# A hybrid transformer block on one core: an even pace for the stream in the scans, the MLP weight's scale two iterations ahead, the MLP's first products ahead of the last norm

## The chip, the cores and the metric

The kernel runs on one core of one Trainium2 chip. Its engines are TensorE (PE; its weight loads are PEld), VectorE (DVE), ScalarE (ACT), GpSimd (POOL) and SyncE (SP, which here issues the DMAs). The metric is the device time of one execution in microseconds (us); less is better.

## The reference, cut to what matters

One layer over 2048 latent tokens and 256 context tokens, with a width D of 1024 and float32 inputs. One projection feeds three mixers (gated linear attention, RWKV-7, retention); their outputs go through one projection, and a squared-ReLU MLP with 4096 hidden columns follows.

```python
zl = modulate(rms_norm(xl, norm1_g), ml[0], ml[1]) @ w_in      # and the same for the context
yl_gla, yl_rwkv, yl_ret = gla_mixer(...), rwkv7_mixer(...), retnet_mixer(...)
xl = xl + ml[2] * (concatenate([yl_gla, yl_rwkv, yl_ret], -1) @ w_out)
hl = modulate(rms_norm(xl, norm2_g), ml[3], ml[4])
xl = xl + ml[5] * (square(relu(hl @ mlp_w1)) @ mlp_w2)
return rms_norm(xl, final_norm_g)
```

## The kernel before

**Stages.** The input projection and the features of RWKV-7 come first (to about 610 us), then the scans (to 2091), the output projection (to 2316) and the MLP.

**The scans** are put in order by a planner, `Order` (L1041). Each piece of work is a generator, a stream with a position that runs from `first` to `last` over `count` yields. `pick` takes, among the streams that are ready by the planner's own clock, the one with the lowest position; one that is more than `lead` ahead of the lowest waits. A yield of a number says how long the stream waits for other engines, and a yield of a function is a condition. The streams are `prepare` and `chains` (RWKV-7's blocks and recurrences), `finish`, `inputs`, `mix` (the heads of the gated attention, then two pairs of retention heads, `ret_pair`, L1654), the finishing of a head, which `follow` (L1776) adds as a stream of its own, and `ip_stream` (L447). The last does what the input projection left open: five groups of columns (`STREAM_T`: V of the attention, its gates, q, k and v of retention pair 0, the same of pair 1, the gates of retention), 16 or 18 token tiles each; a tile is 24 matmuls in four pieces, an eviction (L480) and a store to `zt`. It always is ready, and its positions run from 0 to 312 over 345 pieces. `k.streamed` counts its finished groups. `ret_pair` waits for `streamed >= 3 + p2`; the finishing of a retention pair waits for `streamed >= 5`, all of it. The second pair doesn't begin its queries before the first pair's finishing is done.

**The MLP** takes the tokens in two halves of 1024. Each half has 16 iterations (`fp`) over 256 hidden columns. `hidden` makes seven products `pu` of 12 matmuls each (L2041; a Strassen scheme over 2 x 2 blocks of tokens and columns, `PRODUCTS`), combines them on ScalarE and VectorE (L2049 to L2060), and takes relu and square (L2065, L2066), from which it makes a high and a low part, `uh` and `ul`. Then, for each of 8 token tiles, 12 matmuls into `pz` (L2105) and two sums into `acc` (L2107). In the first half `mlp_w1` (L1857) makes the weights: two loads of 512 KB (`st`, L1866), the largest absolute value (L1867, and across partitions in `over_partitions`: a transpose into `pmx`, L1850, a maximum `mx`, L1852, and a matmul that spreads it, L1853), the scale `s`, and for each product a sum of blocks (`ws`), the high part (L1879), the low part (L1880) and a store to `w1d` (L1881). In the second half they are read back from `w1d`. `wo` has 7 buffers, and the banks of `pu` and `pmx` are four together (pool `mlp1`). `mlp_w2` (L1894) loads and scales the second weight (L1899 to L1905).

**Between them**, `out_proj` (L1918) closes with `norms(7)`, the last two token tiles' norm, then W2, and returns; iteration 0's `hidden` is called in `mlp` (L2025). `norms(7)` works in tiles of the pools `opx` and `opy`; `acc` (pools `mla0` and `mla1`) and `mlx` are opened when these are closed, while `mlu`, `mlw2` and `mlw` lie on the other side of the memory. `norms` for the first 8 token tiles, which is what `hidden` of the first half reads, are done long before.

A scheduler orders each engine's instructions when the kernel is built, with program order as priority, and it moves an instruction ahead of one that isn't ready.

Of the kernel before, what the change touches and what calls it, by code (L numbers as in the profile page):

```python
# [22 lines left out]
P = 128  # L23
# [420 lines left out]
STREAM_T = [TV, TG[0:3], RET_T[0], RET_T[1], TG[3:5]]  # L444


def ip_stream(k, wp, ps):  # L447
# [10 lines left out]
    for g, cols in enumerate(STREAM_T):  # L458
# [4 lines left out]
        for ti in range(2 if kind == "g" else 0, NT):  # L463
# [577 lines left out]
class Order:  # L1041

    def __init__(self, nc):
        self.nc, self.t, self.streams, self.mode = nc, 0.0, [], None

    def add(self, gen, first, last, count, lead=1e9):
        s = Stream(gen, first, last, count, lead)
        s.ready = self.t  # L1050
        self.streams.append(s)
        return s
# [28 lines left out]
    def run(self):  # L1081
# [572 lines left out]
def ret_pair(k, p2, pool, ps):  # L1654
# [6 lines left out]
    nc.sync.dma_start(V.rearrange("p c h n -> p c (h n)"), grp(0, T, vc))  # L1661
# [4 lines left out]
    def keys(t0, n):  # L1666
        c0, nch = t0 // P, n // P
        if t0:
# [13 lines left out]
    yield 4  # L1682
    kd = keys(*TOKB[0])
    yield 4
    for bi, (t0, n) in enumerate(TOKB):
# [15 lines left out]
        if bi + 1 < len(TOKB):  # L1701
            kd = keys(*TOKB[bi + 1])
# [70 lines left out]
    k.fin = follow(k, 5, finish_rows(k, pool, ps, Y, ms, 2, 64, gc, k.col("rng", p2), 768 + 128 * p2))  # L1773


def follow(k, n, gen):  # L1776
# [6 lines left out]
    return k.order.add(steps(), k.mix.pos() - 20, k.mix.pos() + 5, 10)  # L1783


def mixers(k, ps):
# [3 lines left out]
    with tc.tile_pool(name="mix", bufs=1) as mp:  # L1790
# [55 lines left out]
def over_partitions(k, ps, pool, x):  # L1846

    nc = k.nc
    pt = ps.tile([P, 512], F32, tag="p1", name="pmx")
    nc.tensor.transpose(pt[0:1, 0:P], x, k.ident)  # L1850
    m = pool.tile([1, 1], F32, tag="mx1", name="mx1")
    nc.vector.tensor_reduce(m, pt[0:1, 0:P], axis=AX.X, op=ALU.max)  # L1852
    nc.tensor.matmul(pt[:, P : P + 1], k.ones[0:1], m, start=True, stop=True)  # L1853
    return pt[:, P : P + 1]


def mlp_w1(k, fp, sp, tag, bufs, ws, wp, eng):  # L1857

# [404 lines left out]
```

## Time and profile before

| | us |
|---|---|
| median of 3 runs | 3725.27 |
| lowest, highest | 3703.3, 3731.29 |
| the profiled execution | 3744.08 |
| span of its trace, first to last instruction | 3742.3 |

In the rows a line such as `pz<-w2h,uh` names the tile written and the tiles read. Idle time stands before the instruction that ended it, with what released it. The granted clock (PEclk) is TensorE's share of 2.4 GHz; it has two levels, 1.2 and 2.4 GHz, and a share between them is a mean over a stretch.

### The profile page before, as it was taken

How to read it: one execution, taken by the hardware profiler on the slowest of the kernel's cores; microseconds unless marked ns; L12 is line 12 of the kernel's file. 1: busy time of each engine (PE TensorE's matmuls, PEld its weight loads, DVE VectorE, ACT ScalarE, POOL GpSimd, SP SyncE). 2: the span in 40 equal slices, each digit the busy share in tenths (PEclk: the TensorE clock that was granted, in tenths of full speed). 3: DMA queues.
4: the chain of work that ended last, by engine and by line, in shares of the span. 5: the costliest groups of instructions: out<-in, count | busy, mean ns of one | idle time of the engine just before them, and what ended most of it. 6: DMA issues, size and time to landing. Idle time of an engine off the chain costs nothing. (4 is left out here: it accounts for less than half of the span.)

```text
span 3742.3 us, 62893 instructions
## 1 busy us (share of the span) xinstructions
PE 3411.3 (91%) x23616; PEld 2272.0 (61%) x23616; DVE 2437.2 (65%) x5128; ACT 1394.9 (37%) x3097; POOL 685.7 (18%) x863
## 2 busy tenths in 40 slices
PE   6798999999998999989998598899999999999997
PEld 2444446676666766767776486555555556666665
DVE  7458785668856576674665488876777665444446
ACT  3355553344436255252434234333333342112113
POOL 3224443234413222222332100000000010000001
PEclk7898998988978799778888799999999999999998
DMA  7988876446634436333332387633333365223222
GB/s 228 202 229 252 249 214 198 133 135 191 163 115 126 104 105 153 76 102 104 96 98 84 136 201 258 218 130 123 125 124 124 111 184 186 89 89 119 89 89 97
DMA packets 534217, 547.09 MB, mean 146 GB/s; under 512 B 276475, under 2 KB 407366, under 8 KB 533134
## 3 DMA queue, kind: packets, MB, share of 16 engines
q1 hardware_dynamic: 533904, 542.99, 48.7%
q8 instruction: 188, 3.08, 0.4%
q14 instruction: 125, 1.02, 0.1%
HBM read 331.18 MB, written 187.55 MB: 139 GB/s over the span
## 5 line engine op out<-in xcount | busy, mean ns | idle before, releaser
L2041 PE MATMUL pu<-H,wo 128*128 128x512 f16 x2688 | 623.9, 386 | 23.9 <-ACT wo L1879 20.8
L2107 DVE TENSOR_TENSOR acc<-acc,pz 128x512 f32<-128x512 f32 x512 | 348.0, 686 | 376.2 <-PE pz L2105 372.8
L2041 PEld LDWEIGHTS <-wo 128*128 128x128 f16 x2688 | 254.2, 99 | 357.1 <-issue 58.4
L2105 PE MATMUL pz<-w2h,uh 128*128 128x512 f32 x1024 | 441.2, 431 | 26.0 <-ACT uh L2068 23.9
L2105 PE MATMUL pz<-w2l,uh 128*128 128x512 f32 x1024 | 411.4, 402 | 0.0
L2105 PE MATMUL pz<-w2h,ul 128*128 128x512 f32 x1024 | 396.8, 396 | 0.0
L1065 PE MATMUL pz<-rwh,rh 128*128 128x384 f16 (+1 forms) x1376 | 289.3, 342 | 8.5 <-DMA rh<-hd 5.9
L2120 POOL TENSOR_TENSOR acc<-acc,fg 128x1024 f32<-128x1024 f32 x10 | 24.0, 2416 | 1457.6 <-ACT acc L2119 1457.6
L1065 PEld LDWEIGHTS <-rh 128*128 128x128 f16 x2064 | 198.0, 105 | 134.6 <-issue 37.5
L2105 PEld LDWEIGHTS pz<-w2h,uh 128*128 128x128 f32 x1024 | 199.9, 195 | 83.6 <-ACT uh L2068 26.1
L2105 PEld LDWEIGHTS pz<-w2l,uh 128*128 128x128 f32 x1024 | 199.9, 195 | 41.4
L2105 PEld LDWEIGHTS pz<-w2h,ul 128*128 128x128 f32 x1024 | 195.8, 191 | 43.3
L2065 ACT ACTIVATE u<-u 128x512 f32<-128x512 f32 x64 | 36.8, 622 | 476.5 <-DVE s L2059 476.5
L425 PEld LDWEIGHTS <-wh 128*128 128x128 f16 (+2 forms) x1072 | 111.0, 107 | 151.1 <-issue 44.6
L425 PE MATMUL pz<-hT_hi,wh 128*128 128x512 f16 (+5 forms) x536 | 127.2, 379 | 42.0 <-ACT zs L428 23.8
L2053 ACT ACTIVATE s<-pu,iv 128x512 f32<-128x512 f32 x96 | 65.5, 686 | 259.3 <-PE pu L2041 258.0
L1065 PE MATMUL pz<-rwl,rh 128*128 128x384 f16 (+1 forms) x688 | 143.7, 339 | 0.0
L1065 PE MATMUL pg<-Z,BK 64*128 64x128 f32 (+1 forms) x864 | 138.4, 339 | 4.0 <-issue 1.9
L1988 PE MATMUL pz<-woh,yh 128*128 128x512 f32 x256 | 100.2, 406 | 28.2 <-DMA x<-in_w_out_dram 21.6
L1065 PEld LDWEIGHTS pg<-Z,BK 64*128 64x128 f32 x864 | 115.8, 233 | 16.8 <-issue 5.8
L425 PE MATMUL pz<-hT_hi,wl 128*128 128x512 f16 (+5 forms) x536 | 122.8, 366 | 0.0
L425 PE MATMUL pz<-hT_lo,wh 128*128 128x512 f16 (+5 forms) x536 | 121.0, 363 | 0.0
(526 smaller groups left out, 6915.8 us busy)
## 6 DMA issues: line engine op xcount, KB each, us to landing
rh<-hd SPq DMA_DIRECT2D x86, 512.0 KB
st<-in_mlp_w_dram SPq DMA_DIRECT2D x64, 512.0 KB
w1d<-wo SPq DMA_DIRECT2D x112, 256.0 KB
wo<-w1d SPq DMA_DIRECT2D x112, 256.0 KB
x<-in_x_dram SPq DMA_DIRECT2D x32, 512.0 KB
mw<-in_mod_w_dram SPq DMA_DIRECT2D x32, 512.0 KB
w2d<-w2h SPq DMA_DIRECT2D x32, 512.0 KB
w2d<-w2l SPq DMA_DIRECT2D x32, 512.0 KB
```

Of the source, the lines that this page charges most:

```text
L425: nc.tensor.matmul(pz[:M, o : o + step], a[:, kk, 0:M], b[:, kk, t0 + o : t0 + o + step], start=(i == 0), stop=(i == 23))
L1065: return op(out, lhs, rhs, **kw)
L1988: nc.tensor.matmul(pz, a[:, kk], w[:, kk, 512 * hf : 512 * hf + 512], start=(kk + i == 0), stop=(kk == KD - 1 and i == 2))
L2041: nc.tensor.matmul(bank, W[o][:, a, kk], H[o][:, 4 * b + kk], start=(i == 0), stop=(i == 11))
L2053: nc.scalar.activation(s, product(o), AF.Copy, scale=iv)
L2065: nc.scalar.activation(r, r, AF.Relu)
L2105: nc.tensor.matmul(pz, U[q][tb][u][:, ts], W2[q][w][:, cs], start=(i == 0), stop=(i == 5))
L2107: nc.vector.tensor_add(a[:, cs], a[:, cs], pz)
L2120: nc.gpsimd.tensor_mul(a, a, fg)
```

## The change

There are three parts. *The scans*: the gates of retention come fourth and the second retention pair fifth in `STREAM_T`. The stream has a period of 3.1 us of the planner's clock in place of positions: when its next piece is due it goes first; when no other stream is ready it may go up to three periods early. `ret_pair` loads V with the keys, block by block, and waits for the stream's tiles block by block (`there`), not for whole groups; the finishing waits for 4 groups in the first pair and 5 in the second, and its positions begin 10 later. *The scale*: `mlp_w1` is cut in two. `mlp_w1_load` loads the weight two iterations ahead and makes its scale from the sum of squares (on ScalarE, with a matmul that sums across partitions in `norm_scale`, L334); `mlp_w1` is now a generator that makes one product's weight behind each token tile of the iteration before. *The first products*: `hidden` is now `mlp_hidden`, and iteration 0's is called in `out_proj` ahead of W2, and W2 ahead of `norms(7)`; iteration 1's weight is loaded into `mlx`.

```diff
-STREAM_T = [TV, TG[0:3], RET_T[0], RET_T[1], TG[3:5]]
+STREAM_T = [TV, TG[0:3], RET_T[0], TG[3:5], RET_T[1]]
 def ip_stream(k, wp, ps):
...
+            k.tile = ti + 1
             yield 0
-        k.streamed += 1
+        k.streamed, k.tile = k.streamed + 1, 0
...
     def pick(self):
         open_ = [s for s in self.streams if s.cond is None or s.cond()]
+        paced = [s for s in open_ if s.period and s.ready <= self.t]
+        for s in paced:
+            if s.due <= self.t or len(open_) == 1:
+                return s
+        if len(open_) > 1:
+            open_ = [s for s in open_ if not s.period] or open_
         head = min(s.pos() for s in open_)
         near = [s for s in open_ if s.pos() <= head + s.lead] or open_
         ready = [s for s in near if s.ready <= self.t]
         if ready:
             return min(ready, key=Stream.pos)
+        for s in paced:
+            if s.due <= self.t + 3 * s.period:
+                return s
...
+            if s.period:
+                s.due = max(s.due, self.t - s.period) + s.period
...
 def ret_pair(k, p2, pool, ps):
-    nc.sync.dma_start(V.rearrange("p c h n -> p c (h n)"), grp(0, T, vc))
...
     def keys(t0, n):
+        nc.sync.dma_start(V[:, c0 : c0 + nch].rearrange("p c h n -> p c (h n)"), grp(t0, n, vc))
...
-    yield 4
+    def there(i):
+        t0, n = TOKB[i]
+        return lambda: (k.streamed, k.tile) >= (2 + 2 * p2, (t0 + n) // P)
+    yield there(0)
     kd = keys(*TOKB[0])
-    yield 4
+    yield 8
...
         if bi + 1 < len(TOKB):
+            yield there(bi + 1)
             kd = keys(*TOKB[bi + 1])
...
-    k.fin = follow(k, 5, finish_rows(...))
+    k.fin = follow(k, 4 + p2, finish_rows(...))
...
-    return k.order.add(steps(), k.mix.pos() - 20, k.mix.pos() + 5, 10)
+    return k.order.add(steps(), k.mix.pos() - 10, k.mix.pos() + 15, 10)
...
-                yield lambda: k.streamed >= 3 + p2
                 yield from ret_pair(k, p2, pool, ps)
...
-def mlp_w1(k, fp, sp, tag, bufs, ws, wp, eng):
+def mlp_w1_load(k, fp, sp, tag, bufs, jp):
...
         nc.sync.dma_start(st[h], w1v[h, :, :, 256 * fp : 256 * fp + 256])
-        nc.vector.tensor_reduce(am[:, h : h + 1], st[h], axis=AX.XY, op=ALU.max, apply_absolute_value=True)
-    nc.vector.tensor_max(am[:, :1], am[:, :1], am[:, 1:])
-    nc.vector.tensor_scalar(ar, over_partitions(k, k.p1, sp, am[:, :1]), 1e-30, 2.0 ** -14, ALU.max, ALU.mult)
-    nc.vector.reciprocal(s, ar)
-    nc.vector.tensor_mul(iv, ar, k.h_inv2)
+        sq = jp.tile([P, D], BF16, tag="sq", name="sq", bufs=1)
+        nc.scalar.activation(sq.rearrange("p (k n) -> p k n", k=4), st[h], AF.Square, accum_out=am[:, h : h + 1])
+    nc.vector.tensor_add(am[:, :1], am[:, :1], am[:, 1:])
+    s, ar = norm_scale(k, k.p1.tile([P, 512], F32, tag="p1", name="pnrm")[:, 0:1], k.w1s, am[:, :1])
+    nc.vector.tensor_mul(k.iv[:, fp : fp + 1], ar, k.h_inv2)
+    return st, s
+def mlp_w1(k, fp, st, s, sp, ws, wp, eng):
     for o in PRODUCTS:
...
         nc.sync.dma_start(k.w1d[fp, o], w)
+        yield o, w
...
 def out_proj(k, es, H, hp):
...
+        U0 = mlp_hidden(k, H, up, W0, k.iv[:, 0:1])
         k.g2 = mod_row(k, w2, 3)
+        W2 = [mlp_w2(k, q, w2) for q in range(2)]
         norms(7, xs, ss[:, 14:16])
-        W2 = [mlp_w2(k, q, w2) for q in range(2)]
...
 def mlp(k, H, hp, es, U0, W2, up, w2p, wp0):
...
+        loaded = None if half else mlp_w1_load(k, 1, wp, "st", 2, wp)
         for fp in range(NF):
...
-                W1 = mlp_w1(k, fp, (wp, wp0)[fp % 2], "st", 2, 1, k.w1, nc.vector)
                 W2 = [mlp_w2(k, 2 * fp + q, w2p) for q in range(2)]
-            U = hidden(*W1)
+            U = mlp_hidden(k, H, up, W1, k.iv[:, fp : fp + 1]) if fp or half else U0
+            following = iter(()) if half or fp == NF - 1 else mlp_w1(k, fp + 1, *loaded, (wp, wp0)[(fp + 1) % 2], 1, k.w1, nc.vector)
+            if not half and fp < NF - 2:
+                loaded = mlp_w1_load(k, fp + 2, (wp0, wp)[fp % 2], "st", 2, wp)
+            W1 = {}
             for t in range(8):
...
                     nc.vector.tensor_add(a[:, cs], a[:, cs], pz)
+                W1.update([x for x in (next(following, None),) if x])
...
-            k.order.add(ip_stream(k, fp, fps), 0, 312, 345, 4)
+            k.order.add(ip_stream(k, fp, fps), 0, 312, 345, period=3.1)
```

## Rows read from the trace of the kernel before

**Rows 1.** The page's first part: busy us (share of the span) x instructions.
```profile
PE 3411.3 (91%) x23616; PEld 2272.0 (61%) x23616; DVE 2437.2 (65%) x5128; ACT 1394.9 (37%) x3097; POOL 685.7 (18%) x863
```

**Rows 2.** Windows by stage: from:to, length, busy us (instructions) of PE, PEld, DVE, ACT, POOL, granted clock, DMA.
```profile
612.00:2030.00 1418.00, 1320.29 (x13955) 974.29 (x13954) 945.08 (x2549) 596.82 (x1692) 427.49 (x589) 0.86 0.44 123
2030.00:2091.00 61.00, 43.86 (x282) 37.20 (x282) 20.72 (x43) 19.50 (x37) 17.51 (x16) 0.75 0.14 43
...
2316.00:2386.00 70.00, 54.12 (x226) 32.14 (x225) 62.16 (x101) 29.59 (x47) 0.00 (x0) 0.91 0.80 269
2386.00:3006.00 620.00, 563.33 (x2382) 354.34 (x2382) 438.88 (x666) 199.34 (x315) 0.00 (x0) 0.93 0.38 131
...
3075.00:3695.00 620.00, 620.00 (x2782) 399.35 (x2780) 309.93 (x464) 135.00 (x239) 7.50 (x3) 1.00 0.33 113
```

**Rows 3.** Waits of PE, 2386 to 3006: us in total, times, longest us.
```profile
PE pmx L1853 <- DVE mx L1852: 24.6, 13, 2.5
PE pu L2041 <- ACT wo L1879: 20.6, 6, 3.5
PE pz L2105 <- ACT uh L2068: 12.4, 8, 1.6
```

**Rows 4.** Timeline of PE at two iterations' boundaries: start, us, instruction, [idle before].
```profile
2574.23 0.38 PE L1853 MATMUL pmx<-mx,ones 1*128 1x1 f32 x2 [2.49 <-DVE mx L1852]
2578.11 5.46 PE L2041 MATMUL pu<-H,wo 128*128 128x512 f16 x16 [3.50 <-ACT wo L1879]
...
2583.64 0.39 PE L2105 MATMUL pz<-w2l,uh 128*128 128x512 f32 x1
2583.87 0.40 PE L2105 MATMUL pz<-w2h,uh 128*128 128x512 f32 x1
...
2622.36 0.38 PE L1853 MATMUL pmx<-mx,ones 1*128 1x1 f32 x2 [1.96 <-DVE mx L1852]
2624.39 0.79 PE L2105 MATMUL pz<-w2h,uh 128*128 128x512 f32 x1 [1.65 <-ACT uh L2068]
2624.98 0.63 PE L2105 MATMUL pz<-w2l,uh 128*128 128x512 f32 x1
2625.41 0.63 PE L2105 MATMUL pz<-w2h,uh 128*128 128x512 f32 x1
...
2629.90 0.40 PE L2105 MATMUL pz<-w2h,uh 128*128 128x512 f32 x1
```

**Rows 5.** Window between two boundaries of the first half, columns as in Rows 2.
```profile
2624.40:2667.40 43.00, 43.00 (x181) 27.48 (x181) 29.73 (x46) 9.92 (x15) 0.00 (x0) 0.94 0.41 141
```

**Rows 6.** DVE's lines, 2386 to 3006 (busy, mean ns); ScalarE's line L1995 (min/median/max ns).
```profile
L1867 DVE TENSOR_REDUCE am<-st 128x1 f32<-128x1024 f32 x25 | 30.4, 1217 | 9.1 <-DMA st<-in_mlp_w_dram 8.6
...
L1995 ACT ACTIVATE sq<-x x16: 1040/1057/1062, 2137.3 to 2318.1; 128x1024 bf16<-128x1024 f32 x16
```

**Rows 7.** Timeline of SP and DVE: a load of `st` and its reduction.
```profile
2589.18 0.38 SPq L1866 DMA_DIRECT2D st<-in_mlp_w_dram  x1
...
2592.83 1.22 DVE L1867 TENSOR_REDUCE am<-st 128x1 f32<-128x1024 f32 x1 [0.69 <-DMA st<-in_mlp_w_dram]
```

**Rows 8.** Timeline of PE, SP and DVE in the first MLP iteration.
```profile
2333.44 0.80 PE L2105 MATMUL pz<-w2h,uh 128*128 128x512 f32 x1 [8.36 <-ACT uh L2068]
...
2358.86 0.34 SPq L1961 DMA_DIRECT2D h<-hl  x1
...
2361.46 1.92 SPq L2097 DMA_DIRECT2D acc<-x  x4
...
2366.71 1.28 DVE L2107 TENSOR_TENSOR acc<-acc,pz 128x512 f32<-128x512 f32 x2 [2.20 <-DMA acc<-x]
```

**Rows 9.** Line L480 (min/median/max ns, first and last start); timeline of PE in the tail.
```profile
L480 ACT ACTIVATE rzs<-pz,siv x238: 348/368/413, 605.4 to 2021.7; 128x128 f32<-128x128 f32 x119
...
2032.41 1.12 PE L1065 MATMUL fpt<-ident,rY 128*128 128x128 f32 x4 [3.03 <-POOL rY L1463]
...
2083.63 1.11 PE L1065 MATMUL fpt<-ident,rY 128*128 128x128 f32 x4 [7.70 <-POOL rY L1463]
```

More of the change, by code (lines that the diff above doesn't have):

```diff
@@ L1046, in __init__, with add @@
         self.nc, self.t, self.streams, self.mode = nc, 0.0, [], None
-    def add(self, gen, first, last, count, lead=1e9):
+    def add(self, gen, first, last, count, lead=1e9, period=None):
         s = Stream(gen, first, last, count, lead)
-        s.ready = self.t
+        s.ready = s.due = self.t
+        s.period = period
         self.streams.append(s)
@@ L1772, in ret_pair @@
         yield 2
-    k.fin = follow(k, 5, finish_rows(k, pool, ps, Y, ms, 2, 64, gc, k.col("rng", p2), 768 + 128 * p2))
+    k.fin = follow(k, 4 + p2, finish_rows(k, pool, ps, Y, ms, 2, 64, gc, k.col("rng", p2), 768 + 128 * p2))
 def follow(k, n, gen):
@@ L1843, in summed @@
     return out
[L1846 to L1854, printed above, removed]
-def mlp_w1(k, fp, sp, tag, bufs, ws, wp, eng):
+def mlp_w1_load(k, fp, sp, tag, bufs, jp):
     nc = k.nc
@@ L1890, in mlp_w1_kept @@
         k.nc.sync.dma_start(W[o], k.w1d[fp, o])
-    return W, k.iv[:, fp : fp + 1]
+    return W
 def mlp_w2(k, ft, wp):
@@ L1915, in mlp_w2_kept, with mlp_hidden, product, new @@
     return vh, vl
+def mlp_hidden(k, H, up, W, iv):
+    nc = k.nc
+    def product(o):
+        bank = k.p1.tile([P, 512], F32, tag="p1", name="pu")
+        i = 0
+        for a, b in ((0, 0), (1, 0), (0, 1)):
+            for kk in range(4):
+                nc.tensor.matmul(bank, W[o][:, a, kk], H[o][:, 4 * b + kk], start=(i == 0), stop=(i == 11))
+                i += 1
+        return bank
+    def new(nm):
+        return up.tile([P, 512], F32, tag=nm, name=nm, bufs=1)
+    def add(out, o, s):
+        nc.vector.scalar_tensor_tensor(out, product(o), iv, s, ALU.mult, ALU.add)
+    s1, s2, s3 = (new(nm) for nm in ("s1", "s2", "s3"))
+    for o, s in ((1, s2), (2, s3), (0, s1)):
+        nc.scalar.activation(s, product(o), AF.Copy, scale=iv)
+    u10, u01 = new("u10"), new("u01")
+    add(u10, 3, s2)
+    add(u01, 4, s3)
+    nc.vector.tensor_sub(s3, s3, s2)
+    nc.vector.tensor_add(s1, s1, s3)
+    nc.vector.tensor_sub(s2, u10, u01)
+    nc.vector.tensor_add(s2, s2, s1)
+    add(s2, 6, s2)
+    add(s1, 5, s1)
+    U = [[], []]
+    for q, r in ((1, u10), (0, u01), (0, s2), (1, s1)):
+        nc.scalar.activation(r, r, AF.Relu)
+        nc.scalar.activation(r, r, AF.Square)
+        uh = up.tile([P, 512], F32R, tag="uh", name="uh")
+        nc.scalar.copy(uh, r)
+        ul = up.tile([P, 512], F32R, tag="ul", name="ul")
+        nc.vector.tensor_tensor(ul, r, uh.bitcast(F32), ALU.subtract)
+        U[q].append((uh, ul))
+    return [U[0][::-1], U[1]]
 def out_proj(k, es, H, hp):
@@ L2031, in mlp @@
     ps = es.enter_context(tc.tile_pool(name="mlps", bufs=4, space=PSUM))
-    def hidden(W, iv):
-        def product(o):
-            bank = k.p1.tile([P, 512], F32, tag="p1", name="pu")
-            i = 0
-            for a, b in ((0, 0), (1, 0), (0, 1)):
-                for kk in range(4):
-                    nc.tensor.matmul(bank, W[o][:, a, kk], H[o][:, 4 * b + kk], start=(i == 0), stop=(i == 11))
-                    i += 1
-            return bank
-        def new(nm):
-            return up.tile([P, 512], F32, tag=nm, name=nm, bufs=1)
-        def add(out, o, s):
-            nc.vector.scalar_tensor_tensor(out, product(o), iv, s, ALU.mult, ALU.add)
-        s1, s2, s3 = (new(nm) for nm in ("s1", "s2", "s3"))
-        for o, s in ((1, s2), (2, s3), (0, s1)):
-            nc.scalar.activation(s, product(o), AF.Copy, scale=iv)
-        u10, u01 = new("u10"), new("u01")
-        add(u10, 3, s2)
-        add(u01, 4, s3)
-        nc.vector.tensor_sub(s3, s3, s2)
-        nc.vector.tensor_add(s1, s1, s3)
-        nc.vector.tensor_sub(s2, u10, u01)
-        nc.vector.tensor_add(s2, s2, s1)
-        add(s2, 6, s2)
-        add(s1, 5, s1)
-        U = [[], []]
-        for q, r in ((1, u10), (0, u01), (0, s2), (1, s1)):
-            nc.scalar.activation(r, r, AF.Relu)
-            nc.scalar.activation(r, r, AF.Square)
-            uh = up.tile([P, 512], F32R, tag="uh", name="uh")
-            nc.scalar.copy(uh, r)
-            ul = up.tile([P, 512], F32R, tag="ul", name="ul")
-            nc.vector.tensor_tensor(ul, r, uh.bitcast(F32), ALU.subtract)
-            U[q].append((uh, ul))
-        return [U[0][::-1], U[1]]
     NF, ENDS = DFF // 256, (1, 3, 5, 7)
@@ L2224, in tile_hybrid_block @@
             fps = es.enter_context(tc.tile_pool(name="iprps", bufs=1, space=PSUM, side="right"))
-            k.order, k.inputs, k.streamed, k.fin = Order(nc), 0, 0, None
+            k.order, k.inputs, k.streamed, k.tile, k.fin = Order(nc), 0, 0, 0, None
             rw_scan(k, bp, ps)
```

15 lines of the change are left out of this document (6 added, 9 removed).

## The prediction

> **What bounds the kernel now.** The page comes first: TensorE is busy for 91% of the span and VectorE for 65% [rows 1], so TensorE's waits and its clock decide, and the question is in which stage it waits. The table of windows by stage answers that [rows 2]. In the second half of the MLP TensorE is busy for all of 620 us at a granted clock of 1.00 (2.4 GHz) and issues 2782 matmuls: 620 / 2782 = 0.2229 us each. One iteration is 84 products into `pu` and 96 into `pz`, 180 x 0.2229 = 40.1 us. The first half computes the same with weights that it makes itself, and 13 of its iterations take the 620 us from 2386 to 3006: 47.7 us each, at a clock of 0.93. The 13 x 7.6 = 98.4 us between the two halves are the largest sum in reach. The waits of that stretch say where they lie: 24.6 us before `pmx` on `mx`, 20.6 before `pu` on `wo`, 12.4 before `pz` on `uh`, 57.6 in all, 4.4 an iteration [rows 3]. The timeline shows that they all stand at one place, between the last product of an iteration and its first `pz` [rows 4]: TensorE waits 2.49 us for the maximum and then 3.50 for the scaled weight, or, every second time, 1.96 and 1.65. After it the matmuls start 0.43 us apart, which is the 1.2 GHz level, where later ones start 0.23 apart: 13 of them take 2624.39 to 2629.90, 5.5 us in place of 2.9. So a boundary costs 4.4 us of idle time, 0.7 of `pmx` work and 2.6 of slow clock. Between two boundaries nothing else holds TensorE: 181 matmuls fill 43.0 of 43.0 us with VectorE at 69% [rows 5].
>
> In the scans TensorE is busy for 1320 of 1418 us, and then comes a tail of 61 us with 43.9 us of work [rows 2]. The stream's last eviction starts at 2021.7; only then does the first retention pair's finishing start (`fpt` at 2032.41), the second pair's queries wait for that, and its own finishing is the last thing, behind a wait of 7.7 us [rows 9].
>
> **The change part by part.** *The scale.* Two reductions on VectorE, 1.217 us each [rows 6], go, with the maximum across partitions. In their place stand two squares with a sum on ScalarE, the same operation on a tile of the same size as L1995, 1.06 us [rows 6], one small matmul (as `pmx`, 0.5 us) and seven VectorE operations on one column for five that go. Per iteration VectorE falls from 438.9 / 13 = 33.8 us to about 31.5, and ScalarE rises from 199.3 / 13 = 15.3 to about 17.5, with 41 us to do it in [rows 2]: hidden. If they weren't, ScalarE's 2.1 us would be the price. What counts is where the chain stands. It was load, maximum, two matmuls, scale, weight, product; now the scale of iteration n+2 is asked for at the head of n, and the weights of n+1 are made behind each token tile's `pz`. A load takes 3.65 us from issue to the reduction that waited for it [rows 7], and the 96 `pz` take 96 x 0.2229 = 21.4, so the weight is there when the last product of n ends, and the first products of n+1 can fill the wait for `uh`. That is how the second half runs, with weights loaded ahead and no wait at all [rows 2]. Of the 98.4 us I keep 0.5 x 13 = 7 for the small matmul and 0.5 x 13 = 6 for waits that stay, between 0.1 (43.0 - 2.6 slow - 181 x 0.2229 [rows 5]) and the 1.65 of `uh` [rows 4]. The term is **-85**, with bounds -75 to -92.
>
> *The first iteration.* Its products now stand ahead of the last norm and of the weight W2. TensorE waited 8.36 us for `uh` there [rows 8], since VectorE did norm and W2 work in between; 4.0 us (from the end of the last product, 2622.36 - 1.96, to `pz` at 2624.39 [rows 4]) is what that chain takes undisturbed: gain 4.4. Against it: the norm comes later, and what lies where its tiles lay comes later too. Before, the loads of token tiles 4 to 7 of `acc` are issued at 2361.46, right behind the norm's last store at 2358.86, and VectorE waits for them until 2366.71 [rows 8]. TensorE filled that time with the next iteration's products, because their weights were in the pool `mlw`. Now the weights of iteration 1 are loaded into `mlx`, which opens when the norm's pools close. With 8 sums done and 4 banks full, TensorE has 72 `pz` (16 us) before it must stand: from about 2333.4 - 4.4 + 16 + 2.6 = 2348 to between 2359 (8 us of VectorE work on the next weight are out of the norm's way) and 2367. After that 24 `pz` and 84 products, 24 us, lead to 2383 to 2391 and, with a wait for the new scale, some us more, where before the next `pz` block began near 2386. I take **+4**, with bounds -8 and +20: nearer the lower end, as the upper one needs a norm that gains nothing.
>
> *The scans.* The stream's matmuls stay the same; they come every 3.1 us of the planner's time and, between, where nothing else is ready. The gates of the retention heads are streamed ahead of the second pair, so the first finishing no longer waits for the whole stream, and the second pair's queries run beside the recurrences. No price row exists for a new order. Bounds: the tail's 61 us can at best shrink to the last finishing, 2075.9 (2083.63 - 7.70) to 2091, 15 us: -46; with its 43.9 us of work set among holes that are all too short it gains 61 - 44 = 17; and a worse pace can lose. The largest waits for the stream's own loads are a few us, so I bound the loss by the idle time growing by a quarter of 98 us: +25. I take **-25**, near the middle of the gains. Eight more loads of V stand on SP's queue, under 0.5 us each (four `acc` loads took 1.92 [rows 8]), over 200 us: hidden; 4 us if not.
>
> The sum is -85 + 4 - 25 = -106 on the execution of 3744.08 us (span 3742.3). That execution is 0.5% above the median of the runs, 3725.27; off the median the forecast is **3619 us**.
>
> **The rivals.** *The gap stays.* If no weight or no free bank of the four in `p1` is there when the last product ends, TensorE waits 4.0 us for `uh` and starts slowly, as now every second time; idle time changes by 0.4 us an iteration, 5 in all: 3725 - 5 + 4 - 25 = 3699. For it: the scale's tile takes one of the four banks just there. Against: the second half has the same four banks and no gap [rows 2]. The Trainium skill, "Perfetto Trace Analysis" (Identifying the Most-Contended Engine), says that a gap which repeats can mean too few buffers for the next tile; by that rule the gap would stay and the sum be this rival's.
>
> *VectorE paces.* 31.5 us at the 69% that it reached beside a full TensorE [rows 5] would make an iteration of 45.6 us, a gain of 27: 3677. Against: from 2316 to 2386 it was busy for 62.2 of 70 us [rows 2].
>
> *The stream's pace loses*: +25 in place of -25: 3669.
>
> *The other side: the small matmul waits.* It stands in TensorE's queue behind the last product. If the tile's two loads began only there, TensorE would stand for 2 x 3.65 + 2 x 1.06 + 0.15 = 9.6 us and start slowly: 40.1 + 0.5 + 0.5 + 2.6 + 9.6 = 53.3 an iteration, +73: 3725 + 73 + 4 - 25 = 3777. With the other two terms it is slower by 1% from a wait of 8.4 us on. Against: the tiles are free once the weights of n are made, a whole product block (84 x 0.2229 = 18.7 us) earlier. By the Trainium skill, "TensorE: Matmul & The Clock Gate" (Part 2, Step-by-step), matmuls stay in program order and only weight loads are pulled ahead, so such a wait could not be stepped over; the trace agrees, with 2.49 us of nothing before `pmx` [rows 4].
>
> **How the numbers follow.** Less than 1% (37 us) can't be told from no change: the three runs lie 28 us apart. Likeliest, as summed: 0.62, from 3725 - 92 - 8 - 46 = 3579 to about 3665 (MLP -75, first iteration +20, scans -5). VectorE paces 0.12 (3677), the stream's pace loses 0.09 (3669), the gap stays 0.09 (3699), the small matmul waits 0.04 (3777), something worse in the scans 0.04. Below 3688 lie the first three and a little of the fourth: faster 0.85, same 0.10, slower 0.05. The range 3572 to 3682 leaves out the last three and the fringe of the first, under 0.2.
>
> **What would show it.** Right: in the first half an iteration near 41 us at a clock of 1.00, no wait before the small matmul, and `pu` matmuls between the last product and the first `pz`; `fpt` rows of the first pair well before the stream's last eviction, and a tail under 45 us; a new wait of some 10 us on `acc` near 2350. Wrong: boundaries that still show `pz` waiting 4 us for `uh` with matmuls 0.43 us apart behind, or more idle time in the scans than 98 us.

## The result, and the profile after

| | before | after |
|---|---|---|
| median of 4 runs, us | 3716.55 | 3631.61 |
| lowest, highest, us | 3703.3, 3731.29 | 3604.11, 3642.57 |
| the profiled execution, us | 3744.08 | 3641.55 |
| its span, us | 3742.3 | 3639.4 |

The ratio is 0.9743, with a 95% interval of 0.9687 to 0.9800: faster by 117 to 74 us, 96 in the middle, where 106 were forecast. The sum was close. Its terms were less so: two of them erred by 15 and 12 us against each other, and the third, that of the scans, came out right by luck, for a wrong reason.

The page's first part, after (for [rows 1]):
```profile
PE 3362.6 (92%) x23600; PEld 2257.2 (62%) x23600; DVE 2388.7 (66%) x5128; ACT 1427.0 (39%) x3161; POOL 685.8 (19%) x863
```
Windows by stage of after, columns as in [rows 2]: the scans, their tail behind the stream's last eviction, the first MLP iteration, the first half, the second half:
```profile
612.00:2073.80 1461.80, 1357.18 (x14237) 1011.04 (x14235) 963.87 (x2595) 615.66 (x1732) 447.06 (x605) 0.84 0.43 120
1980.00:2073.80 93.80, 76.24 (x372) 64.24 (x372) 43.87 (x134) 27.03 (x59) 19.96 (x20) 0.51 0.14 42
...
2315.90:2385.00 69.10, 46.03 (x187) 29.67 (x188) 51.92 (x88) 27.21 (x44) 0.00 (x0) 0.85 0.81 258
2385.00:2915.00 530.00, 529.87 (x2389) 341.11 (x2389) 403.79 (x661) 223.15 (x362) 0.00 (x0) 1.00 0.42 147
3000.00:3620.00 620.00, 616.28 (x2756) 403.11 (x2754) 307.33 (x465) 135.30 (x240) 4.75 (x2) 1.00 0.29 98
```
The fourth of these lines is the main result. TensorE is busy for 529.87 of 530 us at a granted clock of 1.00, where [rows 2] had 563 of 620 at 0.93. None of the waits of [rows 3] is left, and neither is the slow start behind them [rows 4]. The third line is the price: 46 us of work in 69.1 us. These are the longest waits of TensorE from 2300 to 2385 (us in total, times, longest):
```profile
PE pnrm L338 <- DMA acc<-x: 13.2, 1, 13.2
PE pnrm L338 <- DVE am L1876: 8.8, 1, 8.8
PE pz L2123 <- ACT uh L1965: 7.3, 1, 7.3
```
And this is where the first two stand on TensorE's timeline:
```profile
2335.43 0.39 PE L2123 MATMUL pz<-w2h,ul 128*128 128x512 f32 x1
2349.06 0.56 PE L338 MATMUL pnrm<-am,ones 128*128 128x1 f32 x2 [13.24 <-DMA acc<-x]
...
2374.71 1.03 PE L1938 MATMUL pu<-H,wo 128*128 128x512 f16 x4
2384.49 0.59 PE L338 MATMUL pnrm<-am,ones 128*128 128x1 f32 x2 [8.75 <-DVE am L1876]
```
`pnrm` is the new small matmul that makes a scale; twice TensorE stands before it. The view names the loads of `acc` as what ended the first wait, but the matmul's own input `am` was written only then too, on VectorE's timeline:
```profile
2348.80 0.16 DVE L1876 TENSOR_TENSOR am<-am 128x1 f32<-128x1 f32 x1 [0.48 <-ACT sq L1875]
```
Nothing behind this matmul could have run either: the next `pz` needed a bank that the sums into `acc` freed from 2348.91 on, and iteration 1's products need the weights that this very scale makes. So the first wait is iteration 1's weight coming late. SyncE's timeline says why. It shows the two loads of iteration 2's weight at 2300.72 and the two of iteration 1's, the one that is wanted first, at 2340.07, when the norm's tiles are closed:
```profile
2300.72 1.82 SPq L1873 DMA_DIRECT2D st<-in_mlp_w_dram  x2
...
2340.07 0.98 SPq L1873 DMA_DIRECT2D st<-in_mlp_w_dram  x2
2341.09 2.58 SPq L2115 DMA_DIRECT2D acc<-x  x4
```
To compare stages, the table counts the 5760 `pu` and `pz` matmuls of the MLP, of which the traces of these kernels hold all, and takes the time at the 85th, at the 265th and at the 2881st, where half of them are done. The 85th is the first `pz` in every kernel but first_back, where products of iteration 1 come ahead of it. The table covers before, after, scans_only and the experiments that touch the MLP. All stages are in us; "w_out" is the start of TensorE's wait of some 22 us for that weight, where the scans end.

| kernel | scans end (w_out) | to the 85th | 180 matmuls on | 2616 matmuls on | to the end |
|---|---|---|---|---|---|
| before | 2091.2 | 242.2 | 52.4 | 688.0 | 668.5 |
| after | 2073.8 | 242.1 | 69.0 | 587.5 | 667.0 |
| scans_only | 2045.2 | 241.2 | 53.3 | 683.6 | 668.2 |
| mlp_only | 2065.5 | 240.2 | 66.5 | 586.1 | 670.9 |
| first_back | 2065.6 | 287.2 | 40.5 | 585.4 | 667.1 |
| w1_in_mlw | 2042.9 | 244.6 | 59.7 | 585.5 | 669.3 |
| w2_late | 2060.7 | 246.5 | 48.4 | 589.7 | 667.0 |
| one_ahead | 2052.0 | 238.3 | 69.1 | 681.8 | 667.3 |
| weights_at_head | 2059.4 | 243.0 | 68.2 | 587.5 | 665.4 |
| max_two_ahead | 2058.6 | 245.6 | 69.9 | 606.0 | 671.0 |

Between before and after: -17.4 in the scans, +16.6 - 0.1 around the first iteration, -100.5 in the first half, -1.5 behind it, together -102.9, the difference of the spans. 2616 matmuls are 14.5 iterations, so one takes 47.3 us before and 40.4 after.

### The profile page after: what moved, and what is told of

Read it like the earlier page. It is cut to its first block, busy times and chain, and to the rows that moved or that the text cites. A ratio compares the mean times of both kernels' runs of the same rounds, so it can differ in the third digit from the quotient of the medians.

```text
span 3639.4 us, 62904 instructions
## 1 busy us (share of the span) xinstructions
PE 3362.6 (92%) x23600; PEld 2257.2 (62%) x23600; DVE 2388.7 (66%) x5128; ACT 1427.0 (39%) x3161; POOL 685.8 (19%) x863
## 5 line engine op out<-in xcount | busy, mean ns | idle before, releaser
L1938 PE MATMUL pu<-H,wo 128*128 128x512 f16 x2688 | 608.7, 380 | 1.2 <-DVE s L1946 1.2
L2123 PE MATMUL pz<-w2h,uh 128*128 128x512 f32 x1024 | 425.2, 419 | 11.7 <-ACT uh L1965 10.5
L2123 PE MATMUL pz<-w2l,uh 128*128 128x512 f32 x1024 | 403.4, 394 | 0.0
L425 PEld LDWEIGHTS <-wh 128*128 128x128 f16 (+2 forms) x1072 | 111.5, 108 | 148.5 <-issue 40.8
```

The lines of the kernel that those rows point to most:

```text
L425: nc.tensor.matmul(pz[:M, o : o + step], a[:, kk, 0:M], b[:, kk, t0 + o : t0 + o + step], start=(i == 0), stop=(i == 23))
L1938: nc.tensor.matmul(bank, W[o][:, a, kk], H[o][:, 4 * b + kk], start=(i == 0), stop=(i == 11))
L2123: nc.tensor.matmul(pz, U[q][tb][u][:, ts], W2[q][w][:, cs], start=(i == 0), stop=(i == 5))
```

## The experiments

**The parts alone.** `scans_only` is the kernel before with all hunks of the diff that lie in the scans, `mlp_only` the kernel before with all the others.

> The kernel before with the scans' part of the change alone. Theory (the terms of the sum add up, and in the changed kernel's trace the scans' part is the 17.4 us by which the wait for w_out begins earlier, 2073.8 against 2091.2): that wait begins within 6 us of 2073.8, the MLP is as before, and the time is 17 us lower (3700, ratio 0.995). The prediction's own term said -25 (3692). Rival (the 17 us belong to one pair of profiles and not to the change): the wait begins within 6 us of 2091 and the ratio's interval holds 1.000 in its middle.

Ratio 0.9943 [0.9912, 0.9973]: -21 us, between -33 and -10. The wait for w_out began at 2045.2, not within 6 us of 2073.8: the size held, the place did not. That is a matter of method. Four kernels among others have one and the same program up to the end of the scans (after, first_back, w1_in_mlw, w2_late), and these are their windows from 612 us to that end, columns as before (after stands above). First first_back:
```profile
612.00:2065.60 1453.60, 1346.54 (x14238) 1006.33 (x14238) 964.20 (x2595) 615.50 (x1733) 445.90 (x605) 0.86 0.43 121
```
The same window of w1_in_mlw:
```profile
612.00:2042.90 1430.90, 1326.43 (x14238) 990.90 (x14238) 965.89 (x2595) 615.76 (x1732) 447.50 (x605) 0.86 0.44 123
```
And of w2_late:
```profile
612.00:2060.70 1448.70, 1341.35 (x14238) 1002.38 (x14238) 965.88 (x2595) 616.26 (x1732) 445.25 (x605) 0.86 0.43 122
```
That is 1431 to 1462 us for the same instructions, with TensorE's idle time at 104.5 to 107.4 in all four. What differs is the busy time, 1326 to 1357, with the granted clock. So one pair of profiles can't price a change in the scans below some 30 us; the ratios of timed runs can. Behind the scans the stages of unchanged code agree within some 6 us from kernel to kernel ("to the end" in the table: 665.4 to 671.0).

> The kernel before with the MLP's two parts (scale, first products) and the scans as before. Theory: the parts add up, so this one is faster by 102.9 - 17.4 = 85.5 us (3631, ratio 0.977), with the wait for w_out near 2091 as before, the same two waits of some 13 and 9 us before the small matmul of the scale in the first two iterations, and 40.4 us an iteration after them. Rival (the transition's waits come from what the scans leave behind, not from the MLP's own order): the two waits are below 5 us in all, and it is faster by about 100 us (3617).

Ratio 0.9708 [0.9637, 0.9778]. In the trace everything behind the wait for w_out takes 1563.7 us against 1651.1, -87.4 (after: -85.5). The two waits are there, 12.86 and 6.13 us, and an iteration takes 40.3 us. The wait for w_out began at 2065.5 and not near 2091: once more the same scans at another speed. The first theory held: the waits of the first iteration are the MLP's own.

**What of the scale pays.** Three kernels, each with one thing of it undone. `one_ahead`:
```diff
-            if not half and fp < NF - 2:
-                loaded = mlp_w1_load(k, fp + 2, (wp0, wp)[fp % 2], "st", 2, wp)
+            if not half and 0 < fp < NF - 1:
+                loaded = mlp_w1_load(k, fp + 1, (wp, wp0)[fp % 2], "st", 2, wp)
```
(and the call stands ahead of `following`, which uses it.)

> The changed kernel, but the load and the scale of iteration n+1 are asked for at the head of n (one ahead), not of n-1; the weights are still made one product behind each token tile. In the changed kernel 264 matmuls into the MLP to the start of the second half take 587.5 us, 40.4 an iteration, and the small matmul stands some 3 us behind its input. Theory 1 (the distance of two is what pays): the small matmul's input is late by several us in each iteration, TensorE waits there and starts at the lower clock: 42 to 46 us an iteration, the stretch 610 to 670, the time 25 to 80 us higher. Theory 2 (what pays is that the weights of n+1 are made inside n, and the tiles' turn sets when the load can start whoever asks for it): the stretch within 6 us of 587.5, no wait over 1 us.

46.9 us an iteration, 681.8 us for the stretch, ratio 0.9914 [0.9880, 0.9947]: nearly all of the MLP's gain is gone. That is the first theory, a little over its bounds of 46 and 670; the way is not the one it gave. The waits of TensorE from 2360 to 3000:
```profile
PE pu L1938 <- ACT wo L1889: 41.4, 7, 8.8
PE pz L2123 <- ACT uh L1965: 28.2, 7, 5.1
```
One boundary on VectorE's timeline:
```profile
2521.01 0.16 DVE L1876 TENSOR_TENSOR am<-am 128x1 f32<-128x1 f32 x1 [0.45 <-ACT sq L1875]
```
And on TensorE's:
```profile
2543.69 0.81 PE L1938 MATMUL pu<-H,wo 128*128 128x512 f16 x3
2544.34 0.28 PE L338 MATMUL pnrm<-am,ones 128*128 128x1 f32 x2
2550.26 1.03 PE L1938 MATMUL pu<-H,wo 128*128 128x512 f16 x2 [5.64 <-ACT wo L1889]
```
The small matmul's input `am` was ready at 2521.2, and the matmul ran at 2544.3, 23 us later: it stood in TensorE's queue behind the iteration's products. It didn't wait, but the scale, the weights and the next products waited for it. No run moves this one matmul alone ahead of the products, so that its place is the cause is read from this trace. In the changed kernel it stands in the middle of the products, on its timeline at 2627.68 for an input that VectorE began to write at 2624.18:
```profile
2627.02 0.82 PE L1938 MATMUL pu<-H,wo 128*128 128x512 f16 x3
2627.68 0.28 PE L338 MATMUL pnrm<-am,ones 128*128 128x1 f32 x2
2627.82 0.59 PE L1938 MATMUL pu<-H,wo 128*128 128x512 f16 x2
```
Its scale is for the iteration after next, so its place among the products costs nothing.

`weights_at_head` makes the weights at once at the head of their iteration, with the scale two ahead:
```diff
+            if fp and not half:
+                W1 = dict(mlp_w1(k, fp, *loaded, (wp, wp0)[fp % 2], 1, k.w1, nc.vector))
+                loaded = ahead
...
-                loaded = mlp_w1_load(k, fp + 2, (wp0, wp)[fp % 2], "st", 2, wp)
+                ahead = mlp_w1_load(k, fp + 2, (wp0, wp)[fp % 2], "st", 2, wp)
...
-                W1.update([x for x in (next(following, None),) if x])
```

> The changed kernel with the scale still two iterations ahead, but all seven products' weights of n made at the head of n, as before the change, not one behind each token tile of n-1. Theory 1 (both parts are needed: the scale early, and the weights spread): the wait on wo of before (20.6 us in 13 iterations, and uh behind it) comes back, 42 to 45 us an iteration, the stretch from the 264th matmul to the second half 610 to 655 in place of 587.5, time 25 to 65 us higher. Theory 2 (the early scale alone takes the gap away; the scheduler moves the weights into idle time by itself): the stretch within 6 us of 587.5.

587.5 us, the same to a tenth, ratio 0.9699 [0.9669, 0.9730]; from 2375 to 2905 TensorE has one wait, of 0.7 us. The second theory held: the generator that spreads the weights behind the token tiles contributes nothing here. Where the scale is known in time, the weights go into idle time of ScalarE and VectorE wherever they are asked for in this program.

`max_two_ahead` keeps the place and puts the old way of making the scale back:
```diff
-        nc.scalar.activation(sq.rearrange("p (k n) -> p k n", k=4), st[h], AF.Square, accum_out=am[:, h : h + 1])
+        nc.vector.tensor_reduce(am[:, h : h + 1], st[h], axis=AX.XY, op=ALU.max, apply_absolute_value=True)
```
and with the maximum of `over_partitions` in place of the sum across partitions.

> The changed kernel with the scale made as before, from the largest absolute value on VectorE (two reductions of 1.22 us, a transpose, a maximum and a small matmul an iteration), but still two iterations ahead. Theory 1 (the place of the scale is what pays, not the way it is made): the stretch from the 264th matmul to the second half is 587.5 plus two small matmul groups in place of one, some 590 to 600, and the time within 12 us of the changed kernel's. Theory 2 (VectorE paces: it is busy 404 of 530 us in the changed kernel's steady part, and 2.3 us an iteration more together with a second link through it make TensorE wait for the maximum): over 42 us an iteration, the stretch over 612, time 25 us higher or more.

606.0 us, 41.7 an iteration, between the two theories; ratio 0.9759 [0.9733, 0.9785]. Its steady part, as a window:
```profile
2375.00:2905.00 530.00, 521.54 (x2317) 330.69 (x2316) 415.94 (x643) 191.77 (x304) 0.00 (x0) 0.99 0.40 141
```
And TensorE's only line of waits there:
```profile
PE pu L1951 <- DVE s L1959: 8.5, 6, 2.2
```
By the releaser named there, a product waits for a bank that VectorE has not yet read. So the new way of making the scale is worth 18.5 us, which the prediction had not priced. In the 530 us of this window the waits are 8.5 us, and the transposes and matmuls into `pmx` take 8.2 us where `pnrm` takes 3.7 in the changed kernel. How much belongs to the two reductions and how much to the maximum across partitions, no run separates. VectorE need not be full for such waits: it is busy for 416 of 530 us here and for 404 in the changed kernel.

**The first iteration.** `first_back` undoes the third part alone:
```diff
-        U0 = mlp_hidden(k, H, up, W0, k.iv[:, 0:1])
         k.g2 = mod_row(k, w2, 3)
-        W2 = [mlp_w2(k, q, w2) for q in range(2)]
         norms(7, xs, ss[:, 14:16])
+        W2 = [mlp_w2(k, q, w2) for q in range(2)]
...
-            U = mlp_hidden(k, H, up, W1, k.iv[:, fp : fp + 1]) if fp or half else U0
+            U = mlp_hidden(k, H, up, W1 if fp or half else U0, k.iv[:, fp : fp + 1])
```

> The changed kernel with iteration 0's products and W2 put back behind the last norm; iteration 1's weight still goes into mlx. Theory 1 (the 13 us wait before the small matmul comes from iteration 1's weight: it is loaded into a pool that opens only when the norm's tiles are closed, 40 us behind iteration 2's weight): the wait stays, over 8 us, and the time is within 6 us of the changed kernel. Theory 2 (the order of products, W2 and norm makes the transition's loss of 16.5 us): the wait before the small matmul goes below 3 us and the time is 10 to 17 us lower (3615 to 3622).

Ratio 0.9725 [0.9652, 0.9798], the same as the changed kernel within the intervals. In the table the two stages around the first iteration take 327.7 us against 311.1 after and 294.6 before. The wait before the small matmul did not go; it grew to 40.46 us, on TensorE's timeline:
```profile
2290.95 0.40 PE L2043 MATMUL pz<-woh,yst 128*128 128x512 f32 x1
2331.81 0.56 PE L338 MATMUL pnrm<-am,ones 128*128 128x1 f32 x2 [40.46 <-DVE am L1876]
2332.23 1.01 PE L1938 MATMUL pu<-H,wo 128*128 128x512 f16 x2
```
Now the matmul stands ahead of all 84 products of iteration 0, whose weights were ready from 2231 on, and its own input came at 2331.6, since the loads were issued at 2322.60, behind the norm. That a matmul can't be stepped over is what the Trainium skill, "TensorE: Matmul & The Clock Gate" (Part 2, Step-by-step), says; this trace agrees, with 40.46 us in front of 84 ready products. So the wait is the first theory's, and iteration 1's weight is its cause. By these two traces moving the products forward is worth 16.6 us as long as that weight comes from `mlx`; the timed runs, with medians 7 us apart, are too few to show it.

`w1_in_mlw` exchanges the pools: iteration 1's weight goes into `mlw`, which is there during the norm.
```diff
-        loaded = None if half else mlp_w1_load(k, 1, wp, "st", 2, wp)
+        loaded = None if half else mlp_w1_load(k, 1, wp0, "st", 2, wp0)
...
-                loaded = mlp_w1_load(k, fp + 2, (wp0, wp)[fp % 2], "st", 2, wp)
+                loaded = mlp_w1_load(k, fp + 2, (wp, wp0)[fp % 2], "st", 2, wp0)
```

> The changed kernel with the two pools swapped: iteration 1's weight and its squares go into mlw, which is there since the output projection, iteration 2's into mlx. Theory 1 (the pool is the cause): the small matmul of iteration 1 no longer waits, products of iteration 1 fill the wait for acc, the second wait of 8.75 us (iteration 3's scale, loaded into the same tiles as iteration 1's weight) shrinks with it, and the time is 10 to 18 us lower than the changed kernel's (3614 to 3622). Theory 2 (order of products, W2 and norm): no change, within 4 us. Theory 3 (the loads of acc for token tiles 4 to 7 end the wait, and the weights can't be made in time beside the norm): the wait moves from the small matmul to pz, still over 8 us, and the time is within 5 us.

Ratio 0.9696 [0.9652, 0.9740]; 304.3 us around the first iteration, 6.8 less than after. None of the three theories in full: the wait moved on to the next small matmul, that of iteration 2, whose weight now comes from `mlx`, on TensorE's timeline:
```profile
2306.42 0.39 PE L2123 MATMUL pz<-w2h,ul 128*128 128x512 f32 x1
2320.49 0.55 PE L338 MATMUL pnrm<-am,ones 128*128 128x1 f32 x2 [13.67 <-DMA w1d<-wo]
2320.90 0.59 PE L1938 MATMUL pu<-H,wo 128*128 128x512 f16 x1
```
`w2_late` adds to it that iteration 2's scale is asked for behind the products of iteration 1:
```diff
+            if not half and fp == 1:
+                loaded = mlp_w1_load(k, 2, wp, "st", 2, wp0)
             following = ...
-            if not half and fp < NF - 2:
+            if not half and 0 < fp < NF - 2:
```

> The kernel w1_in_mlw (iteration 1's weight in mlw, iteration 2's in mlx) with iteration 2's load and scale asked for behind the products of iteration 1, so that their small matmul stands behind them in TensorE's queue. In w1_in_mlw that matmul stood 13.67 us for a weight that could only be loaded when mlx opened. Theory 1 (the place of the small matmul in the queue is the cause): no wait over 3 us before it, 65 products fill the wait for acc, the first pz to the start of the second half take 630 to 636 us in place of 645.2 (changed kernel: 656.5), and the time is 8 to 14 us lower than w1_in_mlw (3608 to 3615). Theory 2 (the weights of iteration 1 can't be made beside the norm): the wait moves to a product that waits for wo, over 8 us, and the time stays within 4 us.

Ratio 0.9636 [0.9604, 0.9668], 3608 us; 294.9 us around the first iteration, as before the change (294.6). The 49 us behind its first `pz`, as a window:
```profile
2307.00:2356.00 49.00, 44.43 (x187) 29.26 (x188) 42.59 (x75) 23.75 (x40) 0.00 (x0) 0.92 0.79 247
```
And TensorE's waits from 2300 to 2385:
```profile
PE pnrm L338 <- DVE am L1876: 13.8, 2, 9.2
```
None of this is iteration 2's matmul any more, which now runs without a wait; the second wait is iteration 3's, on TensorE's timeline:
```profile
2350.32 0.28 PE L338 MATMUL pnrm<-am,ones 128*128 128x1 f32 x2
2355.17 0.58 PE L338 MATMUL pnrm<-am,ones 128*128 128x1 f32 x2 [4.57 <-DVE am L1876]
```
From 2325.30 to 2340.90 65 products of iteration 1 fill the time in which `pz` waits for `acc`: the first theory held. The 9.2 us, before iteration 1's matmul, stand where the products' `uh` was waited for anyway, 7.34 in the changed kernel; the 4.57 is the rest of the loss. The first `pz` to the second half take 638.1 us (forecast 630 to 636), against 656.5 after and 740.4 before. It is the fastest kernel of the study.

**What of the scans pays.** `order_only` has the scans' part without the period (first diff), `pace_only` has it with the old order of the groups and the old condition of the finishing (second diff); the MLP is as before. Both keep the part's other hunks: keys and V block by block, and the finishing's later positions.
```diff
-            k.order.add(ip_stream(k, fp, fps), 0, 312, 345, period=3.1)
+            k.order.add(ip_stream(k, fp, fps), 0, 312, 345, 4)
```
```diff
-STREAM_T = [TV, TG[0:3], RET_T[0], TG[3:5], RET_T[1]]
+STREAM_T = [TV, TG[0:3], RET_T[0], RET_T[1], TG[3:5]]
...
-        return lambda: (k.streamed, k.tile) >= (2 + 2 * p2, (t0 + n) // P)
+        return lambda: (k.streamed, k.tile) >= (2 + p2, (t0 + n) // P)
...
-    k.fin = follow(k, 4 + p2, finish_rows(...))
+    k.fin = follow(k, 5, finish_rows(...))
```

> The kernel before with the scans' new order alone: the gates of retention ahead of the second pair, keys and values of a pair block by block, the earlier finishing; the stream keeps its positions (0 to 312) and has no period. The whole scans' part gave a ratio of 0.9943 [0.9912, 0.9973], some -21 us. Theory 1 (what helps is that the finishing and the second pair no longer wait for the whole stream): -12 to -21 us, ratio 0.994 to 0.997, and TensorE's idle time from 612 us to the wait for w_out near 105 us, as with the whole part, against 109 to 115 before. Theory 2 (the pace helps): within 6 us of before, ratio 0.998 to 1.002, idle time near 112.

> The kernel before with the pace of the scans' part, and the groups of the stream in the old order (the second pair before the gates, both finishings behind the whole stream); keys and values block by block as in the change. Theory 1 (the order helps): within 6 us of before, ratio 0.998 to 1.002. Theory 2 (the pace helps): -12 to -21 us, ratio 0.994 to 0.997, idle time near 105 us.

The order without the pace is slower, 1.0055 [1.0026, 1.0084], +20 us. The pace without the order is faster, 0.9883 [0.9851, 0.9916], -44 us, twice what both give together. No theory allowed for a loss. The hunks that both kernels keep were not run alone; if the three effects simply add up, they are worth about 20 - 44 + 21 = -3 us, the order costs 23 and the pace brings 41. Windows from 612 us to the scans' end and from the stream's last eviction to it, of order_only:
```profile
612.00:2083.10 1471.10, 1345.24 (x14234) 999.80 (x14234) 967.27 (x2589) 614.08 (x1728) 441.11 (x603) 0.86 0.42 120
1992.80:2083.10 90.30, 67.75 (x426) 54.73 (x425) 44.69 (x140) 28.14 (x63) 21.02 (x22) 0.67 0.13 41
```
The same two of pace_only:
```profile
612.00:2036.90 1424.90, 1318.92 (x14238) 976.36 (x14238) 954.92 (x2598) 615.80 (x1734) 447.95 (x606) 0.88 0.44 124
1945.90:2036.90 91.00, 73.00 (x472) 59.99 (x468) 44.88 (x164) 35.36 (x77) 19.33 (x20) 0.67 0.15 49
```
TensorE's idle time is 125.9 us with the order alone, 106.0 with the pace alone, 106.1 with both (1433.2 - 1327.1 in scans_only), and 110.8 to 114.9 without either (mlp_only and before). The rest of the pace's gain lies in busy time, which single profiles don't resolve; the timed runs do, since each has its mean granted clock on record. Over pace_only's six runs that is 0.9185 and over the 17 runs of before beside them 0.9084: 0.9084 / 0.9185 = 0.9890, nearly the whole ratio of the times. With the order alone it is 0.9054 over 12 runs, 0.9084 / 0.9054 = 1.0033, over half of the loss. So nearly all of what the pace gains goes with a higher clock.

Last, the size of the period, on top of w2_late, 2.9 and 3.3 in place of 3.1:

> The kernel w2_late (3608 us, ratio 0.9636) with a period of 2.9 in place of 3.1. In all kernels with the new order the scans end 90 to 94 us behind the stream's last eviction, and most of that tail runs at a granted clock of 0.5, since the second pair is what the stream brings last. Theory 1 (that tail is what is left to gain): the last eviction comes over 40 us earlier, the second pair runs beside RWKV-7's last blocks, the scans end 8 to 25 us earlier, ratio 0.957 to 0.961. Theory 2 (the scans are bound by TensorE's work at the clock it is granted, whoever goes first): within 6 us of w2_late, ratio 0.962 to 0.965, with the tail longer by what the stream ends earlier.

> The kernel w2_late with a period of 3.3 in place of 3.1. Theory 1 (the tail behind the stream): the last eviction comes some 40 us later and the scans end 8 to 25 us later, ratio 0.966 to 0.970. Theory 2 (TensorE's work at the granted clock): within 6 us of w2_late, ratio 0.962 to 0.965, and the tail shorter by what the stream ends later.

With 2.9 the ratio is 0.9782 [0.9751, 0.9814], 54 us behind w2_late; with 3.3 it is 0.9691 [0.9657, 0.9725], and its interval overlaps that of w2_late. (The tails that the first expectation puts at 90 to 94 us are 85.4 in scans_only and up to 93.8 in the changed kernel.) The windows as above, of 2.9, with the stretch up to the last eviction between them:
```profile
612.00:2114.10 1502.10, 1390.61 (x14243) 1035.88 (x14242) 973.52 (x2605) 619.18 (x1738) 444.69 (x606) 0.83 0.42 118
612.00:1926.90 1314.90, 1230.65 (x12983) 904.88 (x12982) 871.04 (x2267) 557.07 (x1585) 405.12 (x566) 0.86 0.46 127
1926.90:2114.10 187.20, 159.96 (x1263) 130.99 (x1262) 102.48 (x338) 62.11 (x155) 39.57 (x40) 0.63 0.18 54
```
And of 3.3:
```profile
612.00:2052.60 1440.60, 1323.96 (x14242) 988.71 (x14242) 968.96 (x2605) 617.83 (x1738) 446.30 (x606) 0.87 0.44 123
1963.50:2052.60 89.10, 69.65 (x425) 55.82 (x424) 44.80 (x140) 28.27 (x63) 21.21 (x22) 0.65 0.14 42
```
And the tail of w2_late:
```profile
1970.80:2060.70 89.90, 70.18 (x372) 58.85 (x372) 43.48 (x134) 26.99 (x59) 19.99 (x20) 0.58 0.14 44
```
For 2.9 the first theory has the sign wrong. The stream ends 44 us earlier than in w2_late (1970.8), and the scans end 53 us later. What is left then, 187 us without the stream, runs at a granted clock of 0.63, and the stretch before it at 0.86. Idle time is 111.5 us against 107.4, so nearly all of the loss is busy time: 1390.6 us for the same matmuls that w2_late does in 1341.4, more than the 31 us by which equal programs differ. The timed runs agree: a mean clock of 0.9100 over the five with 2.9 and of 0.9195 over w2_late's four. The second theory is refuted for 2.9 in its "whoever goes first".

What the clock does to matmuls of one form shows in the changed kernel. These are `rpy` of the first retention pair, from 1800 to 1980 with the stream beside it, and of the second pair, from 1980 to 2073.8 without it:
```profile
L1068 PE MATMUL rpy<-rV,rA 128*128 128x64 f32 x64 | 13.3, 292 | 0.0
L1068 PE MATMUL rpy<-rV,rA 128*128 128x64 f32 x64 | 20.5, 424 | 0.7 <-DVE rA L1779 0.7
```
In these traces, then, the clock stays up while the stream's matmuls run among the small ones of the other streams and falls when they are gone. That it would pay to have the stream last to the end is not shown. With 3.3 the last eviction came no later (1963.5, by one profile) and the tail is as long as before; the ratio lies in the range of the first theory and the median, 3612 us, within the second's 6 us of w2_late, so that run decides nothing.

## Why the prediction was right, and where not

**What bounds the kernel.** The first half against the second was the right place to look, and the reason given there held: 57.6 us of waits at the boundaries and the slow clock behind them [rows 3, 4] are all gone.

**The scale, forecast -85, measured -100.5** (mlp_only: -101.9). Mechanism right, size too small. The stretch compared is 14.5 iterations and includes the wait at the start of the second half, 688.0 - 2616 x 0.2229 = 104.9 us above the second half's pace, where the prediction had 98.4 for 13. And of the 13 us kept back for the small matmul and for waits, 4.4 were used (587.5 - 583.1). One step's reason failed: that the weights stand behind each token tile's `pz` plays no part (weights_at_head). One share of the gain was not priced: the way the scale is made is worth 18.5 us (max_two_ahead), where the prediction said that the place of the chain is what counts. And the load's 3.65 us [rows 7], with which the distance of two was argued, decide nothing: in one_ahead the loads were in time, and what was late, by that trace, was the small matmul behind the products in TensorE's queue.

**The first iteration, forecast +4, measured +16.5** (mlp_only +12.1), inside its bounds of -8 to +20. The wait behind 72 `pz` was foreseen, 11 to 19 us long; it came with 13.24. Two things were not. The gain of 4.4 us on `uh` came as 1.0 (8.36 [rows 8] to 7.34), since VectorE still does 2.4 us of work on W2 (2309.07 to 2311.43) ahead of the last products' sums. And iteration 3's weight goes into the tiles of iteration 1's, which was late, so its small matmul stood another 8.75 us with a third slow start behind it. The rival *the small matmul waits*, priced for every iteration and given 0.04, did come true, but only where tiles come free late: in the first iterations.

**The scans, forecast -25, measured -21** [-33, -10]. The number was right and its reason was wrong, so this hit is luck. The prediction laid the gain on the order: finishing and second pair no longer behind the whole stream. It read `fpt` at 2032.41 [rows 9] as the first pair's start. It is the last of four blocks; the line's own summary of before, from 1900 to 2100, begins earlier, and the third block stands ahead of the stream's last eviction at 2021.7:
```profile
L1065 PE MATMUL fpt<-ident,rY x32: 272/421/477, 1989.8 to 2090.7; 128*128 128x128 f32 x32
2017.32 0.60 PE L1065 MATMUL fpt<-ident,rY 128*128 128x128 f32 x4
```
So before the change three of the four blocks (1989.85, 1996.21 and 2017.32) were already under way while the stream still ran, and there was little for the order to free. The other half of the reason failed too, that the second pair's queries run beside the recurrences. The stream now brings that pair last, and in the changed kernel the first transpose of its queries starts 16 us behind the last eviction at 1980.0 and 11 us behind the last matmul of the recurrences (`py`, 1984.7); before the change it came 14 us behind the last eviction (2035.8 against 2021.7):
```profile
1996.05 1.08 PE L1068 MATMUL rpt<-ident,rqr 128*128 128x128 f32 x4 [0.86 <-DVE yny L146]
```
The order costs some 20 us, and the pace, which the prediction treated as a risk, brings over 40. "A tail under 45 us" did not show: it has 93.8 us, at a clock of 0.51.

**The rivals.** *The gap stays* fell: banks and buffers are as they were, four and seven, and the gap is gone. The rule of the Trainium skill that stood beside it, "Perfetto Trace Analysis" (it is found under Optimization Strategy), that a repeating gap can mean too little room for the next tile, does not fit this trace: the gap of 4.4 us an iteration was a late scale and no lack of buffers. *VectorE paces* fell (40.4 us, not 45.6); with the reductions kept it would have been true by a small part (41.7). *The stream's pace loses* fell at 3.1 and would have held at 2.9.

**Still open.** pace_only's order of the groups was not run together with w2_late; from 0.9883 against 0.9943 one would estimate some 20 us below 3608, but these two intervals only just part and come from different sets of runs. Why the new order costs idle time, 125.9 us against 110.8 to 114.9, was not followed up; nor was it run without the block-by-block keys.

## What to carry to other kernels

A matmul that needs a value from a load, a reduction or a pool that opens late should stand in TensorE's queue behind all work that is ready, and its result should be wanted an iteration later; both too early (14 us of standing in w1_in_mlw and 40 in first_back) and too late (a scale 23 us behind its input) cost more than the matmul. Filler work beside small matmuls should not be finished early: ending it 44 us sooner lost 54 us. When the throttled clock moves one stage by 30 us from run to run, price changes there by repeated timings of one part alone, and count matmuls to compare the stages that are steady.

## What the runs showed of the hardware

Behind the stream's last eviction TensorE is busy for 76.24 of 93.8 us, and its granted clock is 0.51, almost always the 1.2 GHz level; before that, with the stream's matmuls among the others, the scans have 0.87 (612 to 1980). The prediction had counted the tail in idle time, 17.6 us here; the clock costs more, an estimated 37 us if all of the 76.24 ran in proportion to it (76.24 x 0.51 = 38.9). The same instructions of the scans took 1431 to 1462 us in four executions, with idle times within 3 us of each other.
